# Unread identity products behind the work that precedes TensorE's pauses, in a two-block kernel on one core

## Chip, core and metric

The kernel runs on one core of one Trainium2 chip. The metric is the device time of one execution in microseconds (us). TensorE (PE) multiplies, VectorE (DVE) and ScalarE (ACT) do elementwise work and empty the product banks, GpSimd (POOL) takes powers, and SyncE (SP) issues the transfers from memory.

## What is computed

The input is 256 positions of width 1024, in float32. A first block mixes (RWKV recurrence, gated linear recurrence), attends to a memory of 256 rows and ends in a convolutional feed-forward layer. A second block does this twice: feed-forward, three-branch token mixing, cross attention, feed-forward. Each step starts from a normalised input:

```python
x = x + merged @ w_mix_out[l]
x = x + cross_attention(rms_norm(x, norm_x_g[l]), rms_norm(mem, norm_mem_g[l]), w_cq[l], w_ckv[l], w_co[l])
x = x + conv_ffn(rms_norm(x, norm_ffn_g[l]), ...)
...
for l in range(DEPTH_2):
    x = x + 0.5 * rms_norm_2(swiglu(h, ffn1_w13[l], ffn1_w2[l]), ffn1_norms[l, 1])
    x = x + rms_norm_2(y, mix_norms[l, 1])                               # y: token mixing
    x = x + rms_norm_2(cross_attention_2(h, m, cross_wq[l], cross_wkv[l], cross_wo[l]), cross_norms[l, 1])
    x = x + 0.5 * rms_norm_2(swiglu(h, ffn2_w13[l], ffn2_w2[l]), ffn2_norms[l, 1])
```

## The kernel before

All weights stream once from memory. `weights` (L213) loads one 512 KB tile `raw`; ACT casts it to a rounded half `wh` (L209) and DVE subtracts to get the rest `wl` (L210). Activations are kept as such pairs too (`xth`, `xtl`). `mm3` (L240) then makes each product from three: high by high, high by low, low by high (L242 to L244). Tiles `raw`, `wh` and `wl` come from rings of buffers, of three each in most steps.

Product banks are of 128 by 512 numbers. `bank` (L132) gives them out from two rings of two: tag `p` for projections (`bp` in the profile), tag `c` for transposes and attention (`bc`). A ring is handed out in the order in which the program is written: the third request waits until the first bank's last user is through. The four accumulators of a down projection (`acc`) are separate.

`norm_T` (L355) opens each step. It normalises the two tiles of 128 positions, `xn` on DVE (L351), and transposes them (L368) with the constant identity `ident` on TensorE, eight transposes to a tile, four to a `bc` bank; ACT and DVE empty each bank into `xth` and `xtl`. Only then can the step's projections run.

What TensorE does meanwhile is set by the scheduler: it simulates the program and queues, engine by engine, what it finds ready, so work that stands later in the code can go ahead of work that waits. In `cross` (L492) this is the projection of the memory (keys and values, `w_ckv` or `cross_wkv`, written after `norm_T`): chunks that were not made in an earlier step, 48 products each with 512 columns. There are two such chunks in the first block and one in each of the two layers of the second. Feed-forward steps are given projections of the memory as `fill`, except the very last one, which has none.

`rwkv` (L643) does the recurrence for two halves of the heads. At the end of each half it transposes the result `yc` (L868); ACT and DVE then scale it, add to it, and split it into `zh` and `zl`, which the branch projection reads.

Of the kernel before, what the change touches and what calls it, by code (L numbers as in the profile page):

```python
# [8 lines left out]
F32 = mybir.dt.float32  # L9
# [7 lines left out]
D = 1024  # L17
# [93 lines left out]
class Core:  # L111
# [87 lines left out]
    def setup(self):  # L199
        nc = self.nc  # L200
        self.x0 = self.load_x(self.a["x"][0], lambda: setattr(self, "g0", self.gvec(self.a["norm_mix_g"][0])))
        self.load_const(["ident"])
        self.ident = self.cst["ident"]
        self.mhalf = self.const.tile([128, 8], F32, name="mhalf")
        nc.vector.memset(self.mhalf, -0.5)


    def split(self, src, h, l):
# [31 lines left out]
    def mm3(self, out, a, b, start, stop):  # L240
        mm = self.nc.tensor.matmul
        mm(out, a.h, b.h, start=start, stop=False, skip_group_check=True)  # L242
        mm(out, a.h, b.l, start=False, stop=False, skip_group_check=True)  # L243
        mm(out, a.l, b.h, start=False, stop=stop, skip_group_check=True)  # L244

    def mm(self, out, a, b, start=True, stop=True):
        self.nc.tensor.matmul(out, a, b, start=start, stop=stop, skip_group_check=True)  # L247

    def fm_pair(self, b, name, bufs):

# [25 lines left out]
    def down(self, acc, t, hid, w, first, last):  # L276
        for half in range(2):
            s = slice(half * 512, (half + 1) * 512)
            self.mm3(acc[t][:, s], hid[:, t * 128:(t + 1) * 128], w[:, s], first, last)

    def down_steps(self, src, nk, pool, ntail):

# [69 lines left out]
                                                op0=ALU.mult, op1=ALU.mult)  # L352
        return xn

    def norm_T(self, xs, gsrc, dst=None, g=None):  # L355

        nc = self.nc
        g = g or self.gvec(gsrc)
        xns = [self.normed(xs[t], g) for t in range(2)]
        xt = dst  # L360
        for t, xn in enumerate(xns):
            if xt is None:
                xt = [Pair(self.s4([128, 4, T], F32R, "xth"), self.s4([128, 4, T], F32R, "xtl")) for _ in range(2)]
            for half in range(2):
                b = self.bank("c")
                for j in range(4):
                    k = half * 4 + j
                    nc.tensor.transpose(b[:, j * 128:(j + 1) * 128], xn[:, k * 128:(k + 1) * 128], self.ident)  # L368
                d = xt[half][:, :, t * 128:(t + 1) * 128]
                self.last_copy = self.split(b.rearrange("p (k c) -> p k c", k=4), d.h, d.l)  # L370
        return [xt[k // 4][:, k % 4, :] for k in range(KD)]
# [31 lines left out]


    def ffn(self, xs, gsrc, w_in, w_out, hidden, fill=None):
        xt = self.norm_T(xs, gsrc)
        if fill:
            self.parts = PK
            fill()
        self.parts = PF  # L410
        pend = []
        with self.pool("ff", 3) as pool, self.pool("tail", FTAIL) as tail, self.pool("raws", 7) as raws:
            self.phase(pool)
            acc, step = self.down_steps(w_out, 2 * NJ, tail, FTAIL)
            for j in range(NJ + 1):
                self.raws = raws if j else self.wp
                if j < NJ:
                    bg = self.proj_fm(self.wcols(w_in, j * 256, 256), xt)
                    bu = self.proj_fm(self.wcols(w_in, FF + j * 256, 256), xt)
                    hd = hidden(j, bg, bu)  # L420
                    if j == 0:
                        self.R("gap0", [128, 48], bufs=1)
                    p = Pair(self.R("hh", [128, 2, T], F32R), self.R("hl", [128, 2, T], F32R))
                    if j == 0:
                        self.R("gap1", [128, 16], bufs=1)
                    self.split(hd, p.h, p.l)
                    pend.append(p)
                if j:
                    for i in range(2):
                        step(2 * (j - 1) + i, pend[j - 1][:, i, :])  # L430
        self.raws = self.wp
        return acc
# [59 lines left out]
    def cross(self, xs, gx, w_q, w_o, mt, w_kv, raw, mid=None, ntail=TAIL):  # L492

        nc = self.nc
        self.parts = PC
        R = self.R
        xt = self.norm_T(xs, gx)
        after = self.last_copy
        kv = {}

        def get(i):

            got = []
            if i in raw:
                for r in raw[i]:
                    p = Pair(R("kvh", [128, 2, T], F32R, 8), R("kvl", [128, 2, T], F32R, 8))
                    with self.tc.issue_after(after):
                        self.split(r, p.h, p.l)
                    got.append([p[:, 0, :], p[:, 1, :]])
            else:  # L510
                got = [self.fm_pair(b, "kv", 8) for b in self.kv_chunk(mt, w_kv, i)]
            if i < 4:
                kv[i] = got[0]
            else:
                for j in range(2):
                    kv[2 * i - 4 + j] = [got[0][j], got[1][j]]

        outs = {}
        sc, pt = {}, {}

        def scores(h):
            if h == 0:
                R("gap0", [128, 16], bufs=1)
            q = self.fm_pair(self.proj_fm(self.wcols(w_q, h * 256, 256), xt), "cq", 2)
            b = self.bank("c")
            v = b.rearrange("p (a c) -> p a c", a=2)
            for t in range(2):
                for i in range(2):
                    self.mm3(v[:, t, :], q[i][:, t * 128:(t + 1) * 128], kv[h][i], t == 0 and i == 0, t == 1 and i == 1)
            p, rc = self.softmax_bank(v, 2, 256 ** -0.5, R("p", [128, 2, T], bufs=4))  # L530
            for t in range(2):
                nc.vector.tensor_scalar(out=p[:, t, :], in0=p[:, t, :], scalar1=rc[:, t:t + 1], scalar2=None,
                                        op0=ALU.mult)
            sc[h] = p

        def values(h):
            p = sc[h]
            b = self.bank("c")
            for kt in range(2):
                for t in range(2):  # L540
                    o = kt * T + t * 128
                    nc.tensor.transpose(b[:, o:o + 128], p[:, t, kt * 128:(kt + 1) * 128], self.ident)
            if h == 0:
                R("gap1", [128, 96], bufs=1)
            pt = self.fm_pair(b, "pt", 2)
            if h == 0:
                R("gap2", [128, 16], bufs=1)
            b = self.bank("c")
            for i in range(2):
                for kt in range(2):  # L550
                    self.mm3(b[:, i * T:(i + 1) * T], kv[4 + h][kt][:, i * 128:(i + 1) * 128], pt[kt],
                             i == 0 and kt == 0, i == 1 and kt == 1)
            outs[h] = self.fm_pair(b, "kv", 8)

        for i in range(6):
            if i not in raw:
                get(i)
        for h in range(4 + LAG):
            if h < 4:
                for i in (h, 4 + h // 2):  # L560
                    if i in raw and (i < 4 or h % 2 == 0):
                        get(i)
                scores(h)
            if h >= LAG:
                values(h - LAG)
        if mid:
            mid()
        return self.down_all([outs[h][i] for h in range(4) for i in range(2)], w_o, ntail)
# [74 lines left out]
    def rwkv(self, lup, krv, hf, zp):  # L643


        nc, cst, vec, mm = self.nc, self.cst, self.vec, self.mm
# [13 lines left out]
        uc = lambda u: slice(u * 128, (u + 1) * 128)  # L660
# [9 lines left out]
        t, m, y, cl = t01[:, 0], t01[:, 1], t2c[:, 0], t2c[:, 1]  # L670
# [194 lines left out]
        V.tensor_tensor(out=yc, in0=yc, in1=rs.unsqueeze(2).to_broadcast([128, 8, 64]), op=ALU.mult)  # L865
        b = W()
        for q in range(4):
            nc.tensor.transpose(b[:, uc(q)], yc[:, 2 * q:2 * q + 2, :].rearrange("p h c -> p (h c)"), self.ident)  # L868
        z = self.R("i0_%d" % hf, [128, 2, T])
        for i, j in enumerate(js):  # L870
            S.activation(out=z[:, i, :].rearrange("p (a c) -> p a c", a=2),
# [99 lines left out]
    def mix1(self, gate_pool, load, early, side):  # L971

        nc, a = self.nc, self.a
        xt = self.norm_T(self.x0, None, g=self.g0)
        load(["vecs"])
        Rg = self.phase(gate_pool)
        with self.pool("m1") as pool, self.wides():
# [47 lines left out]
    def run(self, out):  # L1025
# [39 lines left out]
        with self.pool("b2") as pool:  # L1065
            self.load_const(["ret"], pool)
            for l in range(2):
# [5 lines left out]
                with self.pool("cr") as cp:  # L1073
                    self.phase(cp)
                    acc = self.cross(xs, n2[l, 0], a["cross_wq_2"][l], a["cross_wo_2"][l], mem["mt"],
                                     a["cross_wkv_2"][l], mem["raw"], mid=(lambda: prepare(1)) if l == 0 else side.close, ntail=TAILS[l])
                xs = self.residual(xs, acc, n2[l, 1])
                acc = self.ffn(xs, a["ffn2_norms_2"][l, 0], a["ffn2_w13_2"][l], a["ffn2_w2_2"][l], self.swiglu_hidden,
                               (lambda: fill(2)) if l == 0 else None)
# [382 lines left out]
```

## Time and profile before

| | before |
|---|---|
| median of 3 runs | 2061.27 us |
| lowest and highest | 2055.84 and 2065.23 us |
| profiled execution, its own time | 2056.62 us |
| its span from first to last instruction | 2054.8 us |
| TensorE busy | 1994.9 us (97% of the span), 14508 products |
| DVE, ACT busy | 1320.3 us (64%), 1093.4 us (53%) |
| mean granted TensorE clock | 0.993 |
| share of TensorE in the chain that ended last | 86% |

A row of the time line gives start, duration, engine, line, operation, output and inputs, and how many were merged (x); in brackets stands the idle time before it and what ended it. Durations of products overlap, so what a product costs in a stream is the distance from start to start. The granted clock is 1.00 at 2.4 GHz and 0.50 at 1.2 GHz.

### The profile page before, as it was taken

How to read it: one execution, taken by the hardware profiler on the slowest of the kernel's cores; microseconds unless marked ns; L12 is line 12 of the kernel's file. 1: busy time of each engine (PE TensorE's matmuls, PEld its weight loads, DVE VectorE, ACT ScalarE, POOL GpSimd, SP SyncE). 2: the span in 40 equal slices, each digit the busy share in tenths (PEclk: the TensorE clock that was granted, in tenths of full speed). 3: DMA queues.
4: the chain of work that ended last, by engine and by line, in shares of the span. 5: the costliest groups of instructions: out<-in, count | busy, mean ns of one | idle time of the engine just before them, and what ended most of it. 6: DMA issues, size and time to landing. Idle time of an engine off the chain costs nothing.

```text
span 2054.8 us, 36137 instructions
## 1 busy us (share of the span) xinstructions
PE 1994.9 (97%) x14508; PEld 1831.4 (89%) x14508; DVE 1320.3 (64%) x2183; ACT 1093.4 (53%) x2014; POOL 45.4 (2%) x65
## 2 busy tenths in 40 slices
PE   7999999999999999999999999999999999998998
PEld 6989978899999998789988999999987899888997
DVE  6896566766675566666677655655576656765555
ACT  5763345655564456654456544544466544554444
POOL 0000000000000001000000000000000000000000
PEclk9999999999999999999999999999999999999999
DMA  6432255666666654436665666656635456645663
GB/s 200 145 120 85 90 188 181 224 189 187 186 217 190 193 174 144 138 113 175 200 203 182 218 194 196 204 184 190 196 117 154 122 159 187 204 154 174 194 193 106
DMA packets 259033, 352.92 MB, mean 172 GB/s; under 512 B 12336, under 2 KB 214448, under 8 KB 258864
## 3 DMA queue, kind: packets, MB, share of 16 engines
q1 hardware_dynamic: 258864, 350.60, 55.3%
q8 instruction: 114, 1.87, 0.4%
q14 instruction: 55, 0.45, 0.1%
HBM read 349.50 MB, written 1.05 MB: 171 GB/s over the span
## 4 chain that ended last, share of the span: by engine, by line
PE 86%; DVE 6%; ACT 3%; DMA 3%; issue 1%; POOL 0%; SPq 0%; DVEq 0%; POOLq 0%; ACTq 0%
PE bp L242 20%; PE bp L243 20%; PE bp L244 19%; PE acc L242 6%; PE acc L243 6%; PE acc L244 6%; PE a L247 3%; DVE wl L210 2%; ACT wh L209 1%; PE bc L247 1%; DMA raw<-in_w_in_dram 1%; PE bc L368 1%; DMA raw<-in_cross_wkv_dram 1%; PE bc L1137 1%; DMA raw<-in_cross_wo_dram 1%
## 5 line engine op out<-in xcount | busy, mean ns | idle before, releaser
L210 DVE TENSOR_TENSOR wl<-raw,wh 128x512 fp32r<-128x512 f32 (+2 forms) x1082 | 797.0, 774 | 523.0 <-ACT wh L209 512.4
L209 ACT CAST wh<-raw 128x512 fp32r<-128x512 f32 (+2 forms) x1082 | 699.7, 688 | 701.4 <-PE bp L243 486.6
L242 PE MATMUL bp<-xth,wh 128*128 128x256 f32 x2704 | 759.7, 281 | 8.1 <-ACT xth L209 4.8
L244 PE MATMUL bp<-xth,wl 128*128 128x256 f32 x2704 | 756.5, 280 | 5.5 <-DVE wl L210 5.4
L243 PE MATMUL bp<-xtl,wh 128*128 128x256 f32 x2704 | 756.8, 280 | 2.7 <-DVE xtl L210 2.7
L242 PEld LDWEIGHTS bp<-xth,wh 128*128 128x128 f32 x2704 | 512.4, 190 | 19.6 <-ACT xth L209 6.4
L244 PEld LDWEIGHTS bp<-xth,wl 128*128 128x128 f32 x2704 | 511.7, 189 | 11.3 <-DVE wl L210 6.9
L243 PEld LDWEIGHTS bp<-xtl,wh 128*128 128x128 f32 x2704 | 511.2, 189 | 6.8 <-DVE xtl L210 4.0
L243 PE MATMUL acc<-wl,hh 128*128 128x512 f32 x440 | 172.9, 393 | 0.0
L244 PE MATMUL acc<-wh,hl 128*128 128x512 f32 x440 | 170.9, 391 | 0.0
L242 PE MATMUL acc<-wh,hh 128*128 128x512 f32 x440 | 142.7, 393 | 0.0
L242 PE MATMUL bp<-wh,xth 128*128 128x512 f32 (+1 forms) x256 | 98.7, 400 | 2.3 <-DVE tmd L1132 1.4
L243 PE MATMUL bp<-wl,xth 128*128 128x512 f32 (+1 forms) x256 | 100.5, 396 | 0.0
L244 PE MATMUL bp<-wh,xtl 128*128 128x512 f32 (+1 forms) x256 | 99.2, 393 | 0.0
L244 PEld LDWEIGHTS acc<-wh,hl 128*128 128x128 f32 x440 | 82.7, 188 | 15.0
L243 PEld LDWEIGHTS acc<-wl,hh 128*128 128x128 f32 x440 | 82.8, 188 | 14.3
L242 PEld LDWEIGHTS acc<-wh,hh 128*128 128x128 f32 x440 | 79.2, 188 | 14.1
L343 POOL TENSOR_TENSOR rr<-rv,mhalf 128x1 f32<-128x1 f32 x46 | 30.1, 656 | 1644.8 <-DVE rv L341 1644.3
L242 PEld LDWEIGHTS bp<-wh,xth 128*128 128x128 f32 x256 | 47.3, 188 | 13.3 <-ACT tmd L1282 2.2
L243 PEld LDWEIGHTS bp<-wl,xth 128*128 128x128 f32 x256 | 48.2, 188 | 9.2 <-DVE wl L210 0.8
L244 PEld LDWEIGHTS bp<-wh,xtl 128*128 128x128 f32 x256 | 48.2, 188 | 8.4
L244 PE MATMUL bp<-bh,wl 128*128 128x256 f32 x192 | 54.0, 281 | 0.0
(377 smaller groups left out, 2578.7 us busy)
## 6 DMA issues: line engine op xcount, KB each, us to landing
raw<-in_ffn_w_dram SPq DMA_DIRECT2D x264, 512.0 KB, 4.4
raw<-in_w_in_dram SPq DMA_DIRECT2D x134, 512.0 KB, 3.7
raw<-in_w_ffn_in_dram SPq DMA_DIRECT2D x44, 512.0 KB, 4.6
raw<-in_cross_wkv_dram SPq DMA_DIRECT2D x32, 512.0 KB, 4.4
raw<-in_w_branch_dram SPq DMA_DIRECT2D x24, 512.0 KB, 3.8
raw<-in_w_ffn_out_dram SPq DMA_DIRECT2D x22, 512.0 KB, 4.2
raw<-in_w_ckv_dram SPq DMA_DIRECT2D x16, 512.0 KB, 4.7
raw<-in_w_out_dram SPq DMA_DIRECT2D x16, 512.0 KB, 4.2
```

The costliest lines, as they stand in the source:

```text
L209: first = self.nc.scalar.copy(out=h, in_=src)
L210: self.nc.vector.tensor_tensor(out=l, in0=src, in1=h.bitcast(F32), op=ALU.subtract)
L242: mm(out, a.h, b.h, start=start, stop=False, skip_group_check=True)
L243: mm(out, a.h, b.l, start=False, stop=False, skip_group_check=True)
L244: mm(out, a.l, b.h, start=False, stop=stop, skip_group_check=True)
L247: self.nc.tensor.matmul(out, a, b, start=start, stop=stop, skip_group_check=True)
L343: nc.gpsimd.tensor_tensor(out=r, in0=v, in1=self.mhalf[:, :1], op=ALU.pow)
L368: nc.tensor.transpose(b[:, j * 128:(j + 1) * 128], xn[:, k * 128:(k + 1) * 128], self.ident)
L1137: self.nc.tensor.transpose(b[0:s.shape[1], i * 128:(i + 1) * 128], s, self.ident)
```

## The change

A new helper `busy` writes products of 128 by 128 into a bank that nobody reads, `ident` by `ident` or ones by ones, by the plain `mm`. It is put at these places:

- in `setup`, 24 products of ones, before anything else;
- in `norm_T`, where asked, after the eighth transpose of each tile: 6 and 2 in the first mixing step and in the feed-forward step without fill (the last one), 4 and 1 in the three cross attentions;
- in `rwkv`, 14 after the last half's transposes;
- in `run`, 22 after the down projection of the last cross attention.

The banks are of ring `p`, except in `setup` and `rwkv`, where they are of ring `c`.

```diff
+        ones = self.s4([128, D], F32, "ones")[:, 0:128]
+        nc.vector.memset(ones, 1.0)
+        self.busy(24, "c", ones)
...
+    def busy(self, n, tag="p", src=None, after=None):
+
+        b = self.bank(tag)
+        src = self.ident if src is None else src
+        with ExitStack() as order:
+            if after is not None:
+                order.enter_context(self.tc.issue_after(after))
+            for _ in range(n):
+                self.mm(b[:, 0:128], src, src)
...
-            self.mm3(acc[t][:, s], hid[:, t * 128:(t + 1) * 128], w[:, s], first, last)
+            self.last_down = self.mm3(acc[t][:, s], hid[:, t * 128:(t + 1) * 128], w[:, s], first, last).ins
...
-    def norm_T(self, xs, gsrc, dst=None, g=None):
+    def norm_T(self, xs, gsrc, dst=None, g=None, busy=0):
...
-                    nc.tensor.transpose(b[:, j * 128:(j + 1) * 128], xn[:, k * 128:(k + 1) * 128], self.ident)
+                    turn = nc.tensor.transpose(b[:, j * 128:(j + 1) * 128], xn[:, k * 128:(k + 1) * 128], self.ident)
+                if busy and half:
+                    self.busy(busy if t == 0 else busy // 3, after=turn.ins)
...
-        xt = self.norm_T(xs, gsrc)
+        xt = self.norm_T(xs, gsrc, busy=0 if fill else 6)
...
-        xt = self.norm_T(xs, gx)
+        xt = self.norm_T(xs, gx, busy=4)
...
+        if hf:
+            self.busy(14, "c", after=turn.ins)
...
-        xt = self.norm_T(self.x0, None, g=self.g0)
+        xt = self.norm_T(self.x0, None, g=self.g0, busy=6)
...
+                if l:
+                    self.busy(22, after=self.last_down)
```

The order in which the engines take their work moves with it. TensorE at the start of the last cross attention, before: projection of the memory (`mth`, `mtl` are its transposed halves), then transposes of the first tile. The 36 products ahead of the first transpose all read `wh`, `wl` of the memory's weights and follow directly on the accumulator products.

```order
L243 MATMUL bp_19594<-wl_19556,mth1_12123 128x512
L244 MATMUL bp_19594<-wh_19555,mtl1_12124 128x512
L368 MATMUL bc_19509<-c_ident_80,xn_19485 128x128 x4
L368 MATMUL bc_19516<-c_ident_80,xn_19485 128x128 x4
L242 MATMUL bp_19569<-wh_19563,mth1_12123 128x512
L242 MATMUL bp_19594<-wh_19563,mth1_12123 128x512
```

The same place now, from the last accumulator product on (lines are those of the changed file: L381 transposes, L250 is `mm`, L245 to L247 are `mm3`).

```order
L246 MATMUL acc11_19371<-wl_19477,mh_19354 128x512
L247 MATMUL acc11_19371<-wh_19476,ml_19355 128x512
L381 MATMUL bc_19575<-c_ident_80,xn_19551 128x128 x4
L381 MATMUL bc_19582<-c_ident_80,xn_19551 128x128 x4
L250 MATMUL bp_19587<-c_ident_80 128x128 x4
L381 MATMUL bc_19594<-c_ident_80,xn_19561 128x128 x4
L381 MATMUL bc_19601<-c_ident_80,xn_19561 128x128 x4
L250 MATMUL bp_19606<-c_ident_80 128x128
L245 MATMUL bp_19642<-wh_19612,mth0_12187 128x512
```

All transposes and the new products stand ahead of the memory's projection, of which nothing is left before them. The other two cross attentions are moved in the same way.

ACT at the program's start, before: splits of transposed tiles (`xth`) between casts of the first weights (`wh`).

```order
L209 CAST xth_110<-bc_114 128x4x128
L209 CAST wh_156<-raw_154 128x1024
L209 CAST xth_112<-bc_121 128x4x128
L209 CAST wh_162<-raw_160 128x1024
L209 CAST xth_110<-bc_128 128x4x128
L209 CAST wh_233<-raw_231 128x1024
```

ACT at the same place now.

```order
L212 CAST wh_193<-raw_191 128x1024
L212 CAST wh_199<-raw_197 128x1024
L212 CAST xth_137<-bc_141 128x4x128
L212 CAST xth_139<-bc_148 128x4x128
L212 CAST wh_270<-raw_268 128x1024
L212 CAST xth_137<-bc_162 128x4x128
```

Two casts of weights now stand ahead of the first split.

## Rows read from the trace of the kernel before

**Rows 1.** Page, busy time of engines; then TensorE's waits: total, times, longest.

```profile
PE 1994.9 (97%) x14508; PEld 1831.4 (89%) x14508; DVE 1320.3 (64%) x2183; ACT 1093.4 (53%) x2014; POOL 45.4 (2%) x65
...
PE acc L242 <- ACT kvh L209: 10.6, 9, 2.8
```

**Rows 2.** Stretches: length, busy PE, PEld, DVE, ACT, POOL (x), granted clock, DMA, GB/s.

```profile
16.64:21.30 4.66, 4.66 (x22) 4.66 (x23) 4.18 (x18) 0.44 (x1) 0.00 (x0) 1.00 0.92 265
21.30:26.00 4.70, 4.70 (x41) 4.53 (x40) 0.72 (x3) 1.33 (x2) 0.00 (x0) 1.00 0.34 115
...
268.98:273.89 4.91, 4.91 (x21) 4.68 (x22) 0.82 (x2) 0.36 (x1) 0.00 (x0) 0.50 0.00 0
1062.37:1065.78 3.41, 3.41 (x18) 3.41 (x18) 1.86 (x4) 0.02 (x1) 0.00 (x0) 0.50 1.03 403
1857.68:1867.92 10.24, 6.51 (x27) 5.69 (x28) 6.81 (x11) 3.73 (x8) 1.12 (x3) 0.50 0.67 241
```

**Rows 3.** Time line of PE at the end of `rwkv`.

```profile
265.06 0.66 PE L868 MATMUL a<-c_ident,i 128*128 128x128 f32 x4 [1.49 <-DVE i L865]
268.98 0.79 PE L242 MATMUL bp<-zh,wh 128*128 128x256 f32 x2 [3.27 <-ACT zh L209]
```

**Rows 4.** Time line of the last feed-forward step's start, DVE and PE.

```profile
1859.07 1.41 DVE L351 SCALAR_TENSOR_TENSOR xn<-x,rr,g 128x512 f32<-128x512 f32 x2
...
1859.96 1.94 PE L368 MATMUL bc<-c_ident,xn 128*128 128x128 f32 x8 [4.80 <-DVE xn L351]
1863.35 1.97 PE L368 MATMUL bc<-c_ident,xn 128*128 128x128 f32 x8 [1.45 <-DVE xtl L210]
1865.14 0.79 PE L242 MATMUL bp<-xth,wh 128*128 128x256 f32 x2
```

**Rows 5.** Last cross attention, PE: time line, then one group of 1775.85 to 1789.2.

```profile
1775.67 0.40 PE L244 MATMUL acc<-wh,ml 128*128 128x512 f32 x1
1775.91 0.40 PE L242 MATMUL bp<-wh,mth 128*128 128x512 f32 x1
...
1791.49 0.38 PE L243 MATMUL bp<-xtl,wh 128*128 128x256 f32 x1 [0.65 <-DVE xtl L210]
...
L242 PE MATMUL bp<-wh,mth 128*128 128x512 f32 x16 | 6.3, 401 | 0.0
```

**Rows 6.** Last cross attention, time line of DVE: the two normalised tiles.

```profile
1780.06 1.42 DVE L351 SCALAR_TENSOR_TENSOR xn<-x,rr,g 128x512 f32<-128x512 f32 x2 [0.43 <-DMA g<-in_cross_norms_dram]
...
1782.21 1.41 DVE L351 SCALAR_TENSOR_TENSOR xn<-x,rr,g 128x512 f32<-128x512 f32 x2 [0.66 <-POOL rr L343]
```

**Rows 7.** Cross attention of the second block's first layer, DVE and PE.

```profile
1049.86 1.41 DVE L351 SCALAR_TENSOR_TENSOR xn<-x,rr,g 128x512 f32<-128x512 f32 x2
...
1061.28 0.39 PE L243 MATMUL bp<-xtl,wh 128*128 128x256 f32 x1 [0.90 <-DVE xtl L210]
```

**Rows 8.** Cross attention of the first block, DVE and PE.

```profile
304.73 0.69 DVE L383 TENSOR_TENSOR x<-acc,x 128x512 f32<-128x512 f32 x1
305.49 1.42 DVE L351 SCALAR_TENSOR_TENSOR xn<-x,rr,g 128x512 f32<-128x512 f32 x2
...
329.52 0.39 PE L242 MATMUL bp<-xth,wh 128*128 128x256 f32 x1 [0.94 <-DVE kvl L210]
```

**Rows 9.** Plain products of 128 by 128: twelve `mm` calls of `pv_tokens` (L1145).

```profile
892.50 2.84 PE L247 MATMUL a<-vt,pt 128*128 128x128 f32 x24
```

**Rows 10.** Program's start: ACT, DVE and PE.

```profile
9.40 0.59 ACT L209 CAST xth<-bc 128x512 fp32r<-128x512 f32 x1
...
12.56 1.04 ACT L209 CAST wh<-raw 128x1024 fp32r<-128x1024 f32 x1 [0.74 <-DMA raw<-in_w_in_dram]
...
15.03 0.69 DVE L210 TENSOR_TENSOR xtl<-bc,xth 128x512 fp32r<-128x512 f32 x1
...
16.64 0.58 PE L242 MATMUL bp<-xth,wh 128*128 128x256 f32 x1 [1.07 <-ACT wh L209]
17.02 0.42 PE L243 MATMUL bp<-xtl,wh 128*128 128x256 f32 x1
```

More of the change, by code (lines that the diff above doesn't have):

```diff
@@ L243, in mm3 @@
         mm(out, a.h, b.l, start=False, stop=False, skip_group_check=True)
-        mm(out, a.l, b.h, start=False, stop=stop, skip_group_check=True)
+        return mm(out, a.l, b.h, start=False, stop=stop, skip_group_check=True)
     def mm(self, out, a, b, start=True, stop=True):
         self.nc.tensor.matmul(out, a, b, start=start, stop=stop, skip_group_check=True)
+    def busy(self, n, tag="p", src=None, after=None):
[6 more added lines that the diff above has]
+                self.mm(b[:, 0:128], src, src)
     def fm_pair(self, b, name, bufs):
@@ L867, in rwkv @@
         for q in range(4):
-            nc.tensor.transpose(b[:, uc(q)], yc[:, 2 * q:2 * q + 2, :].rearrange("p h c -> p (h c)"), self.ident)
+            turn = nc.tensor.transpose(b[:, uc(q)], yc[:, 2 * q:2 * q + 2, :].rearrange("p h c -> p (h c)"), self.ident)
+        if hf:
+            self.busy(14, "c", after=turn.ins)
         z = self.R("i0_%d" % hf, [128, 2, T])
```

## The prediction

> **What bounds the kernel now.** I read the page first: TensorE is busy for 97% of the span, 1994.9 us [rows 1]. Time can therefore come from two places only: the pauses of TensorE, and the stretches in which it works at the lower clock. I looked for the second by the stretches with their granted clock [rows 2]. At 0.50, the 1.2 GHz level, 22 products take 4.66 us at the program's start, 0.212 us each. After the rise 41 take 4.70 us, 0.115 us each. (The clock column still says 1.00 for the start; the spacing of the products shows the lower level.) So a stretch of products at the lower level costs twice its due. Three such stretches lie near edits: 268.98 to 273.89, 1062.37 to 1065.78 and the end of 1857.68 to 1867.92 [rows 2]. Ahead of the first and last lie pauses, 3.27 us [rows 3] and 4.80 us [rows 4]. Next I read the time line of the pauses, and last, against the order in which the engines take their work, who fills the time that the norms take. That reading decides: in the last cross attention TensorE goes from its last accumulator product at 1775.67 straight to the memory's projection at 1775.91 [rows 5], while DVE needs until 1780.06 to begin the first normalised tile [rows 6]. The norm's latency is hidden there, by 36 products.
>
> **The change, part by part.** I number the product of 128 by 128 first. Twelve plain products appear as 24 records with a duration of 2.84 us from first start to last end [rows 9]; less the tail of the last that is 0.22 us each at full clock, and twice that, 0.45 us, at the lower level.
>
> *End of rwkv.* The 14 products take 14 x 0.22 = 3.1 us and start when the four transposes are through, about 265.5. They end near 268.6, before `zh` allows the next real product at 268.98 [rows 3]: nothing is delayed. If the clock holds, the 4.91 us at the lower level [rows 2] become half: **-2.4 us**. Had the clock fallen before, they would take 14 x 0.45 = 6.3 us and delay by 2.9 us, which is the other end (about +0.5 net of the clock, since the run then comes out of it warm).
>
> *Last feed-forward step.* The 22 products take 4.8 us against a pause of 4.80 us [rows 4], so they neither delay nor leave a hole. The transposes after it wait for DVE's split (the 1.45 us [rows 4]), not for TensorE, so a faster clock does little for them, and 6 + 2 products fit between. What is won is the products from 1865.14 [rows 4] to the rise at 1867.92 [rows 2]: 2.78 us become 1.4: **-1.4 us**. Bounds: -2.3 (the transposes too) and +1 (products late).
>
> *Start.* The 24 products of ones start at about 1 us and end between 6.4 us (full clock) and 11.7 us (never). The first splits of `xt` cannot be hurt by that, because ACT's order now has two weight casts ahead of them, and the second of those starts at 12.56, when its transfer has landed [rows 10]. The first split stood at 9.40 [rows 10] and goes to 13.6. From there I follow the chain with DVE's durations: subtraction of both banks until 16.4, the second tile's transposes behind these, its splits on ACT after the cast that ends at 16.6, then DVE's 1.23 us weight subtraction and 0.69 us: the stream that began at 17.02 [rows 10] begins near 18.5. That is 1.5 us late; small later waits for weights give some back: **+1.0 us**, between -1.0 (the 4.66 us at the lower clock [rows 2] shortened after all) and +2.2.
>
> *The three cross attentions.* Here the change moves work. `busy` asks for a `p` bank twice inside `norm_T`, and the memory's projection, later in the code, asks for the next two. The ring has two, so these products must wait until the new ones are through, and the new ones are placed behind the transposes. The order shows it: 36 products ahead of the first transpose before, none now. They are the same products, so nothing is saved: TensorE stands while the norm runs, then makes them. The price of standing I take from the last feed-forward step, the one norm in the trace before that has no cover: from the start of `xn` at 1859.07 to the first projection at 1865.14 it takes 6.07 us, and the first transpose comes 0.89 us after `xn` [rows 4]. The second `xn` comes 2.15 us after the first in the last cross attention [rows 6] and 2.2 us in that step, so the pattern carries over.
>
> - Last cross attention: `xn` at 1780.06 [rows 6], so TensorE stands from 1775.91 to 1780.95, and the memory's 48 products (16 of each kind [rows 5]) start at 1786.1. They are 0.233 us apart (the distance of 1775.67 and 1775.91 [rows 5]), 11.2 us. The pause is as long as the one after which the clock fell [rows 4], so I charge the fall: the run at the lower level after products resume lasted 2.8 to 4.9 us [rows 2, 3, 4], of which half is lost, 1.4 to 2.4, taken 1.9. The projection of `xt` starts at 1799.2 instead of 1791.49 [rows 5]: **+7.7 us**, 5.8 if the clock holds, 8.5 with a stall for the weights behind it.
> - First layer: `xn` at 1049.86 [rows 7], products from 1055.9, 11.2 and 1.9 us, so 1069.0 against 1061.28 [rows 7], 7.7 us; the fall of the clock from 1062.37 on, which cost 3.41 / 2 [rows 2], is then not paid: **+6.0 us**, between 4 and 7.
> - First block: DVE now has the last addition, 0.6 us, ahead of `xn`, which so starts at 306.1 instead of 305.49 [rows 8]. With 6.07 us the projection starts at 312.2; with DVE's new order of the four subtractions, in which the second tile's first bank comes ahead of the first tile's second, at 313.4. Taken 312.8, then 96 products, 22.4 us, and 0.6 us for a clock that may fall: 335.8 against 329.52 [rows 8]: **+6.3 us**, between 5 and 8.5.
>
> On the clock in this last place the Trainium skill ("TensorE: Matmul & The Clock Gate", Part 4) adds a rule: transposes do not count as activity for the clock as products do. The trace agrees so far that eight transposes from 1863.35 were followed by no rise, which came 2.78 us into the products [rows 2, 4]. By the rule the first block's clock would surely fall, and its term would be 1.3 us larger; I leave it.
>
> Give-back: TensorE waits in the later parts of the cross attentions, 10.6 us over nine waits for `kvh` [rows 1]. These hang on ACT's queue, whose casts wait for buffers that TensorE's own products free, so they move along with it: taken 1, up to 4.
>
> Sum: 6.3 + 6.0 + 7.7 + 1.0 - 2.4 - 1.4 - 1 = **+16.2 us**. Against the profiled execution's own 2056.62 us that is 2072.8; that execution is 4.65 us under the median of 2061.27 and lies in the range of the three runs. The mean of all four is 2059.7, and I set the sum on that: **2076 us**.
>
> **The rivals.** *The clock and the later waits pay it back.* The standing TensorE leaves DVE, ACT and the transfers time to run ahead; the 10.6 us of waits for `kvh` [rows 1] shrink to a few, and the clock holds in all three places (-4.4). Then the sum is 16.2 - 4.4 - 5 = +7, 2067 us. For it: these waits exist; against it: the buffers that link both sides.
>
> *Ready products pass the waiting transposes.* If TensorE took the memory's products while a transpose ahead waits, nothing would be lost in the cross attentions and the gains would stand: -2.4 - 1.4 - 1.7 + 1.0 = -4.5, 2055 us; it is decided by whether the queue keeps its order at the first pause of 5 us. The trace speaks against it: the product that ran at 17.02 had its `xtl` by 15.72 and its weights before that, yet it ran behind the one that waited until 16.64 [rows 10]. The Trainium skill ("TensorE: Matmul & The Clock Gate", table at the top) has the queue as a window that pulls weight loads ahead; this case shows nothing of products doing so.
>
> *The products don't hold the clock.* Then they run at 0.45 us: 14 delay by 2.9 us, 22 by some 5 us, the gains of 3.8 go, and the first block pays the clock too: 16.2 + 2.9 + 5 + 3.8 + 1.3 = +29, 2089 us. Against it: they are plain products like those after which the clock rose.
>
> **How the numbers follow.** Forecast 0.68, pay-back 0.18, passing 0.06, no hold 0.08. A measurement of this kernel can tell 0.5%, 10.3 us, from no change: the marks are 2051 and 2071.6. The terms' low ends give 5 + 4 + 5.8 - 1 - 2.4 - 2.3 - 4 = +5, their high ends 8.5 + 7 + 8.5 + 2.2 + 0.5 + 1 = +28, not all at once. The range is 2062 to 2086: it takes in the pay-back and leaves out passing and no hold. Slower: most of the forecast (0.62) and all of no hold, with a little of pay-back, 0.72; within: the rest of forecast and pay-back and most of passing, 0.26; faster 0.02.
>
> **What would show it.** In the profile after, pauses of about 5 us (last layer), 6 us (first layer) and 3 us (first block) in front of the transposes of each cross attention, ended by `xn`; the memory's products behind the transposes in one run; the clock at 1.00 from 265 to 274 and from 1855 to 1868; the first stream of products near 18.5. Wrong would be: no such pauses (passing), or pauses but the next steps starting as early as before (pay-back), or new products 0.45 us apart in the two covered pauses.

## The result, and the profile after

The change makes the kernel slower: the median went from 2057.36 us to 2074.06 us (seven runs of each, 2055.59 to 2065.23 and 2069.59 to 2076.30), a ratio of 1.0071 with a 95% interval of 1.0057 to 1.0084. The forecast was 2076 us, and slower. The profiled execution after took 2076.30 us, with a span of 2074.5 us.

The page first, then TensorE's waits (total, times, longest), as in [rows 1].

```profile
PE 2017.4 (97%) x14690; PEld 1854.6 (89%) x14690; DVE 1321.5 (64%) x2184; ACT 1095.2 (53%) x2014; POOL 45.5 (2%) x65
...
PE bc L381 <- DVE xn L364: 13.5, 3, 5.4
PE acc L245 <- ACT kvh L212: 9.3, 9, 2.2
...
PE bp L245 <- DVE kvl L213: 3.8, 4, 0.9
```

TensorE is again 97% busy, now of a longer span: the average share says nothing. What says something is the new first line of the waits: transposes (L381) wait for `xn` three times, 13.5 us. Before, the long one of them was the 4.80 us of the last feed-forward step [rows 4]; that one is gone, and these three are the cross attentions. Their time line on TensorE, first block, first layer, last layer (last accumulator product, first transpose, first product of the memory, first product of `xt`; in the first block the memory's halves are called `xth` and `xtl` too, and its products are those with 512 columns):

```profile
300.24 0.40 PE L247 MATMUL acc<-wh,ml 128*128 128x512 f32 x1
303.56 1.32 PE L381 MATMUL bc<-c_ident,xn 128*128 128x128 f32 x8 [2.92 <-DVE xn L364]
...
310.70 0.77 PE L245 MATMUL bp<-wh,xth 128*128 128x512 f32 x1
...
325.03 0.51 PE L245 MATMUL bp<-wh,xth 128*128 128x512 f32 x1 [0.94 <-DVE kvl L213]
...
337.25 0.39 PE L245 MATMUL bp<-xth,wh 128*128 128x256 f32 x1 [0.94 <-DVE kvl L213]
...
1051.79 0.39 PE L247 MATMUL acc<-wh,ml 128*128 128x512 f32 x1
1057.31 1.97 PE L381 MATMUL bc<-c_ident,xn 128*128 128x128 f32 x8 [5.13 <-DVE xn L364]
...
1062.78 0.50 PE L245 MATMUL bp<-wh,mth 128*128 128x512 f32 x1
...
1074.99 0.38 PE L245 MATMUL bp<-xth,wh 128*128 128x256 f32 x1 [0.94 <-DVE kvl L213]
...
1788.40 0.39 PE L247 MATMUL acc<-wh,ml 128*128 128x512 f32 x1
1794.23 1.97 PE L381 MATMUL bc<-c_ident,xn 128*128 128x128 f32 x8 [5.44 <-DVE xn L364]
...
1799.69 0.67 PE L245 MATMUL bp<-wh,mth 128*128 128x512 f32 x1
...
1812.07 0.38 PE L245 MATMUL bp<-xth,wh 128*128 128x256 f32 x1 [0.94 <-DVE kvl L213]
```

In [rows 5] the accumulator product at 1775.67 was followed by the memory's product at 1775.91. Now 5.44 us of nothing stand there, and the memory's products come 5.46 us behind the first transpose. The stretches with their granted clock (columns as in [rows 2]), in the order of time: the start, the end of `rwkv`, the three cross attentions, the last feed-forward step:

```profile
1.08:8.42 7.34, 7.34 (x50) 7.34 (x51) 1.57 (x3) 2.83 (x7) 0.56 (x1) 1.00 0.88 283
...
14.94:18.36 3.42, 2.80 (x13) 2.74 (x13) 3.10 (x7) 2.22 (x3) 0.00 (x0) 0.50 1.08 355
18.36:26.00 7.64, 7.34 (x63) 7.06 (x61) 3.81 (x17) 1.66 (x2) 0.00 (x0) 1.00 0.61 148
265.00:268.30 3.30, 3.16 (x28) 2.97 (x27) 1.61 (x3) 1.50 (x3) 0.00 (x0) 1.00 0.30 119
...
305.08:315.32 10.24, 8.15 (x28) 6.49 (x27) 3.85 (x6) 1.76 (x3) 0.00 (x0) 0.50 0.03 12
...
1057.31:1062.84 5.53, 5.53 (x27) 5.49 (x27) 3.63 (x7) 1.86 (x4) 0.55 (x1) 0.50 0.70 214
...
1794.23:1800.11 5.88, 5.88 (x27) 5.85 (x28) 3.98 (x7) 2.22 (x4) 0.55 (x1) 0.50 0.12 43
1875.29:1880.36 5.07, 5.07 (x46) 5.01 (x45) 5.01 (x10) 3.50 (x12) 1.10 (x2) 1.00 0.93 305
1880.36:1888.00 7.64, 6.85 (x54) 6.02 (x54) 4.39 (x8) 2.35 (x4) 0.55 (x1) 1.00 0.56 209
```

The covers of the two old pauses, and the products behind them, are at 1.00 (2.4 GHz) now, where [rows 2] had 0.50. (The column says 1.00 for the very start as well; as in the kernel before, the spacing shows otherwise there: the products of ones are 0.43 us apart until 4.7 us, and 0.22 us after that.) The three new pauses are followed by 0.50 (1.2 GHz): the fall has moved from the places covered to the places made.

To see what each place is worth, I took every product of the old kernel in the trace, subtracted its start from the start of the same product in the other trace, and took the median of that lag in stretches between the places. What the lag grows by at a place is that place's share, in us (what a row lacks to its last column came between the places):

| execution | start | end of rwkv | first block | first layer | last layer | last feed-forward | in all |
|---|---|---|---|---|---|---|---|
| forecast | +1.0 | -2.4 | +6.3 | +6.0 | +7.7 | -1.4 | +16.2 (with -1 given back) |
| the change | -0.9 | -2.0 | +10.1 | +5.6 | +7.6 | -0.5 | +19.8 |
| e1, without the cross attentions' products | -0.3 | -2.2 | +1.5 | +0.5 | +1.0 | -0.7 | -0.4 |
| e2, these in ring `c` | -0.8 | -1.3 | -0.5 | -0.2 | -0.3 | -1.3 | -4.5 |
| e3, two banks of `p` alone | -1.1 | -0.1 | +9.0 | +6.6 | +6.3 | -0.3 | +20.3 |
| e4, new pauses filled too | -1.2 | -1.4 | +7.3 | +7.3 | +5.8 | -0.7 | +17.0 |
| e5, e2 with the later waits filled | +1.6 | -1.3 | +1.5 | -1.1 | +1.1 | -0.7 | +1.0 |
| e6, ring `c` products alone | -0.7 | +0.1 | +1.3 | -1.7 | +0.4 | +0.1 | -0.5 |
| e7, rwkv and last feed-forward alone | +2.0 | -1.3 | -0.9 | -0.5 | -0.4 | -0.7 | -1.0 |
| e8, start alone | -1.6 | -0.7 | -0.5 | -0.1 | +0.4 | +0.6 | -2.0 |
| e9, e7 with e6 | +2.8 | -1.3 | -1.0 | -2.1 | +0.1 | -0.8 | -2.3 |
| e10, e7 once more | +0.2 | -2.2 | -1.3 | +0.4 | +0.3 | -0.7 | -3.3 |

Each row is one execution. Its columns can be off by 1 to 2 us, at the start by up to 3 us, even where nothing was edited (e7 and e10 are one kernel, without the start's products: +2.0 and +0.2 at the start). Terms of that size are read from several rows, and the verdict on a kernel from its ratio.

### The profile page after: what moved, and what is told of

It is laid out like the page before. It is cut to its first block, busy times and chain, and to the rows that moved or that the text cites. A ratio compares the mean times of both kernels' runs of the same rounds, so it can differ in the third digit from the quotient of the medians.

```text
span 2074.5 us, 36505 instructions
## 1 busy us (share of the span) xinstructions
PE 2017.4 (97%) x14690; PEld 1854.6 (89%) x14690; DVE 1321.5 (64%) x2184; ACT 1095.2 (53%) x2014; POOL 45.5 (2%) x65
## 4 chain that ended last, share of the span: by engine, by line
PE 87%; DVE 5%; ACT 3%; DMA 3%; issue 1%; POOL 0%; SPq 0%; DVEq 0%; POOLq 0%; ACTq 0%
PE bp L245 20%; PE bp L246 20%; PE bp L247 20%; PE acc L245 6%; PE acc L246 6%; PE acc L247 6%; PE a L250 4%; DVE wl L213 2%; ACT wh L212 2%; PE bc L250 1%; PE bc L381 1%; DMA raw<-in_cross_wkv_dram 1%; PE bc L1156 1%; DMA raw<-in_w_in_dram 1%; DMA g<-in_cross_norms_dram 1%
## 5 line engine op out<-in xcount | busy, mean ns | idle before, releaser
L245 PE MATMUL bp<-xth,wh 128*128 128x256 f32 x2704 | 757.9, 281 | 5.4 <-DVE kvl L213 2.8
L247 PE MATMUL bp<-xth,wl 128*128 128x256 f32 x2704 | 754.7, 280 | 4.8 <-DVE wl L213 4.8
L245 PEld LDWEIGHTS bp<-xth,wh 128*128 128x128 f32 x2704 | 510.2, 189 | 16.5 <-DVE kvl L213 4.1
L247 PEld LDWEIGHTS bp<-xth,wl 128*128 128x128 f32 x2704 | 508.9, 188 | 10.4 <-DVE wl L213 6.0
L247 PE MATMUL acc<-wh,hl 128*128 128x512 f32 x440 | 170.9, 391 | 0.0
L245 PE MATMUL acc<-wh,hh 128*128 128x512 f32 x440 | 142.8, 393 | 0.0
L245 PE MATMUL bp<-wh,xth 128*128 128x512 f32 (+1 forms) x256 | 99.7, 404 | 2.7 <-DVE tmd L1151 1.4
L247 PE MATMUL bp<-wh,xtl 128*128 128x512 f32 (+1 forms) x256 | 99.5, 395 | 0.0
L247 PEld LDWEIGHTS acc<-wh,hl 128*128 128x128 f32 x440 | 82.7, 188 | 15.1
L245 PEld LDWEIGHTS acc<-wh,hh 128*128 128x128 f32 x440 | 79.2, 188 | 14.1
L245 PEld LDWEIGHTS bp<-wh,xth 128*128 128x128 f32 x256 | 47.9, 190 | 14.2 <-ACT tmd L1301 2.2
L381 PE MATMUL bc<-c_ident,xn 128*128 128x128 f32 x224 | 37.4, 307 | 21.4 <-DVE xn L364 13.5
L247 PEld LDWEIGHTS bp<-wh,xtl 128*128 128x128 f32 x256 | 48.7, 190 | 8.6
```

The lines of the kernel that those rows point to most:

```text
L247: return mm(out, a.l, b.h, start=False, stop=stop, skip_group_check=True)
L381: turn = nc.tensor.transpose(b[:, j * 128:(j + 1) * 128], xn[:, k * 128:(k + 1) * 128], self.ident)
```

## The experiments

**Is it the cross attentions, and there the ring?** Four kernels were run beside the kernel before. The first drops the products there:

```diff
-        xt = self.norm_T(xs, gx, busy=4)
+        xt = self.norm_T(xs, gx)
```

> The changed kernel without the unread products in the three cross attentions; all its other places stay (start, end of rwkv, last feed-forward step). Theory (the two banks taken from ring p move the memory's projection behind the norm): TensorE again makes 36 of the memory's products ahead of the first transpose of the second block's cross attentions, the pauses of 2.9 to 5.4 us there are gone, and what is left are the other terms as the changed kernel's trace shows them, about -2.1 at the end of rwkv, -1.1 at the last feed-forward step and -1 to 0 at the start: 2052 to 2055 us where before is 2057, ratio 0.998 (0.996 to 0.9995). Rival 1 (the loss in the cross attentions has another cause, for instance their transfers or the later waits): 2068 us or more. Rival 2 (the other places cost too): over 2060 us.

Measured: 2056.19 us, ratio 0.9988 (0.9977 to 0.9999). The waits for `xn` are gone from the list, and the rest is a small gain; theory met, both rivals out.

The second keeps the five products of each place, but takes their banks from the other ring:

```diff
+                    self.busy(busy if t == 0 else busy // 3, tag, after=turn.ins)
...
+        xt = self.norm_T(xs, gx, busy=4, tag="c")
```

> The changed kernel with the same unread products in the cross attentions (4 and 1), but their bank taken from ring c instead of ring p; nothing left out. Theory (it is the ring, not the products): the memory's products stand ahead of the transposes again; the five products per step, 1.1 us of TensorE at most in each of three places, and a later transfer of a c bank cost 1 to 4 us together: 2053 to 2058 us, ratio 0.998 to 1.001. Rival (the products or their place behind the transposes cost the time): as slow as the changed kernel, 2070 to 2076 us.

Measured: 2053.19 us, ratio 0.9974 (0.9962 to 0.9985). The same products, placed behind the same transposes, and by the ratios (1.0071 and 0.9974) some 20 us less than the change. Its time line on TensorE in the last cross attention shows why: the memory's products run right up to the transposes, which wait for nothing; the unread products come later, behind the rest of the memory's.

```profile
1780.92 0.40 PE L246 MATMUL bp<-wl,mth 128*128 128x512 f32 x1
1781.15 0.40 PE L247 MATMUL bp<-wh,mtl 128*128 128x512 f32 x1
1781.39 1.03 PE L381 MATMUL bc<-c_ident,xn 128*128 128x128 f32 x8
...
1785.13 1.16 PE L250 MATMUL bc<-c_ident 128*128 128x128 f32 x8
```

The third is the reverse: the kernel before with two banks of ring `p` taken in each cross attention, one product in each, and nothing else of the change.

```diff
-                    self.busy(busy if t == 0 else busy // 3, after=turn.ins)
+                    self.busy(1, after=turn.ins)
```

> The kernel before, with one unread product in each of two p banks in every cross attention, and nothing else of the change. Theory: the two banks alone carry the whole loss of the cross attentions, read as +10.4, +4.9 and +8.5 us by place, with up to 1 us of it given back: less 3 x 3 x 0.22 = 2 us for the products that are fewer, +20 us, 2077 us, ratio 1.0095 (1.008 to 1.0115). Rival (the unread products carry it): four of five are gone, so under +6 us, 2063 us.

Measured: 2080.22 us, ratio 1.0105 (1.0084 to 1.0125). Two products of 0.22 us per place bring the whole loss (four runs, all of them slower than the slowest of the kernel before). On TensorE in the first layer:

```profile
1059.05 1.97 PE L378 MATMUL bc<-c_ident,xn 128*128 128x128 f32 x8 [6.17 <-DVE xn L361]
1060.81 0.63 PE L247 MATMUL bp<-c_ident 128*128 128x128 f32 x2
1062.46 1.97 PE L378 MATMUL bc<-c_ident,xn 128*128 128x128 f32 x8 [1.02 <-DVE xtl L210]
...
1064.51 0.77 PE L242 MATMUL bp<-wh,mth 128*128 128x512 f32 x1
```

With e1 to e3 this is settled: the two banks are the cause, and neither the products in them nor their place. A bank asked for in `norm_T` stands ahead of the memory's in the ring, its user waits for the transposes, and so the memory's products wait for the norm.

**How much of the loss is the clock?** The fourth fills the new pauses as well:

```diff
+        self.busy(24, after=self.last_down)
         xt = self.norm_T(xs, gx, busy=4)
```

> The changed kernel with 24 more unread products in front of each cross attention's norm, behind the last product of the down projection ahead of it, so that TensorE is busy in the new pause. Theory (of the loss, the fall of the clock is a part, the missing cover by the memory's products the rest): the clock stays at 1.00 through 300 to 316, 1051 to 1063 and 1788 to 1800; each place wins half of what runs at 0.50 there, 2.3 us in the first block, 2 to 2.8 in the others: 2067 us (2065 to 2070), ratio 1.005. Rival 1 (the clock is the whole loss): back to 2055 us. Rival 2 (the products don't hold the clock, or are late): 2074 us or more.

Measured: 2070.24 us, ratio 1.0056 (1.0039 to 1.0074). The three places (columns as above) are at full clock:

```profile
298.00:315.00 17.00, 15.45 (x105) 13.82 (x104) 11.26 (x20) 7.32 (x16) 1.12 (x2) 1.00 0.31 97
1049.00:1064.00 15.00, 12.70 (x91) 11.22 (x91) 9.78 (x18) 6.33 (x16) 2.38 (x4) 1.00 0.56 180
1787.00:1801.00 14.00, 12.29 (x90) 10.89 (x89) 11.11 (x21) 6.86 (x19) 2.75 (x4) 1.00 0.34 122
```

But the ratio moves by 1.0071 - 1.0056 = 0.0015, 3 us, not the 7 us that I expected, and the intervals overlap. So the traces speak for the clock as the small part of the loss and the norm without cover as the large one; four runs of e4 do not measure the small part by time. In the first block 2.8 us came back, in the last layer 1.8; in the first layer nothing did, since there the norm itself came later: `xn` waited for the vector `g`, in the change 0.40 us, in e4 1.64 us (DVE, change first, then e4).

```profile
1056.51 1.41 DVE L364 SCALAR_TENSOR_TENSOR xn<-x,rr,g 128x512 f32<-128x512 f32 x2 [0.40 <-DMA g<-in_cross_norms_dram]
```

```profile
1055.34 1.41 DVE L364 SCALAR_TENSOR_TENSOR xn<-x,rr,g 128x512 f32<-128x512 f32 x2 [1.64 <-DMA g<-in_cross_norms_dram]
```

**Is a pause that no work can fill worth covering?** In the cross attentions' later part TensorE waits for `kvh`, and the clock falls. To e2 I added ten products there, in the second block:

```diff
+                    turn = self.mm3(b[:, i * T:(i + 1) * T], kv[4 + h][kt][:, i * 128:(i + 1) * 128], pt[kt],
...
+            if h == 1 and mid:
+                self.busy(10, "c", after=turn.ins)
```

> The kernel of the run with the cross attentions' unread products in ring c, and 10 more unread products (ring c) behind the second head's last values product in the cross attentions of the second block, where TensorE waits for the cast of kvh (2.59 us and 2.34 us in that run) and the clock falls each time. Theory (a pause that nothing useful can fill is worth covering): the products, 10 x 0.22 = 2.2 us, lie in the waits, the clock stays at 1.00 around 1097 to 1101 and 1828 to 1831, each place wins half of 3.41 us: 3.4 us less than 2053.2, about 2050 us, ratio 0.9957 (0.9945 to 0.9972). Rival 1 (the products push back the transposes of p and with them ACT's casts, the wait grows): 2053 us or more, ratio 0.9975 or more. Rival 2 (what follows waits for weights, the faster products wait later): as before, 2053 us.

Measured: 2056.15 us, ratio 0.9995 (0.9985 to 1.0005): no gain over e2, rather a loss. The theory fell. TensorE in the first layer, then in the last, there with ACT's cast that the pause was a wait for:

```profile
1098.05 2.50 PE L250 MATMUL bc<-c_ident 128*128 128x128 f32 x20
1100.60 0.50 PE L245 MATMUL acc<-wh,kvh 128*128 128x512 f32 x1
...
1829.74 0.58 ACT L212 CAST kvh<-bc 128x512 fp32r<-128x512 f32 x1
1829.89 4.13 PE L250 MATMUL bc<-c_ident 128*128 128x128 f32 x20 [1.95 <-ACT p L501]
1833.78 0.48 PE L245 MATMUL acc<-wh,kvh 128*128 128x512 f32 x1
```

In the first layer they lie in the wait, as meant. In the last they wait 1.95 us for ACT's `p` to release their own bank of ring `c`. ACT goes straight from there to the awaited cast of `kvh`, which ends at 1830.32, 0.43 us after the cover's first product. The cover then runs for 4.13 us, most of it at the lower clock (0.50 from 1830.28 to 1833.69), and pushes the awaited product back to 1833.78. So the cover waited for the same stretch of ACT's queue as the product that it was to cover for. What makes e5 slower than e2 beyond that one place was not separated.

**The small parts.** The five products in ring `c` alone:

```diff
+        xt = self.norm_T(xs, gx, busy=4, tag="c")
```

> The kernel before with the five unread products of each cross attention in ring c and nothing else of the change. Theory A (they do nothing; the 2.9 us between the run without them and the run with them in ring c is chance): 2057 to 2061 us, ratio 0.9993 to 1.0008. Theory B (they hold the clock behind the transposes): no stretch at 0.50 near 1062 and 1792, 1.7 us won at the first of these, ratio 0.9980 to 0.9992. Theory C (they cost their own time, 3 x 1.1 us): ratio 1.0015.

Measured: 2056.35 us, ratio 0.9994 (0.9985 to 1.0002): worth nothing that can be told. Theory C is out; A and B are not told apart, since most executions without these products have no fall of the clock near 1062 either.

The products at the end of `rwkv` and in the last feed-forward step alone, run twice:

```diff
+        xt = self.norm_T(xs, gsrc, busy=0 if fill else 6)
...
+        if hf:
+            self.busy(14, "c", after=turn.ins)
...
+                if l:
+                    self.busy(22, after=self.last_down)
```

> The kernel before with the 14 products at the end of rwkv and the 22, 6 and 2 of the last feed-forward step; nothing at the start, nothing in the cross attentions. Theory (the start's products are worth nothing, because a transfer of weights sets the time at 110 us anyway): -2.0 at the end of rwkv and -0.5 to -1.3 at the last step, ratio 0.9983 to 0.9993, as the run with the start's products too. Rival (the start's edit costs its 1 us): ratio 0.9980 or less, and the first 100 us of the trace earlier than there by 1 us.

> The products at the end of rwkv and in the last feed-forward step alone, once more, beside the two other kernels: 0.9976 (0.9967 to 0.9985) if the first value holds; 0.9985 or more if it was a lucky draw and these two places bring only the -2.0 and -0.5 us that the traces show.

Measured: 2053.18 us, 0.9976 (0.9967 to 0.9985), then 2054.08 us, 0.9989 (0.9980 to 0.9998). Both are gains. The first lies below the theory's range, where the rival (the start costs 1 us) had put it; the second lies on the side of the lucky draw, and the run of the start alone (below) does not bear out the rival. The mean, 0.9982, is 3.6 us, a little over the 2 to 3 us that the places show.

The start alone:

```diff
+        ones = self.s4([128, D], F32, "ones")[:, 0:128]
+        nc.vector.memset(ones, 1.0)
+        self.busy(24, "c", ones)
...
+        xt = self.norm_T(self.x0, None, g=self.g0, busy=6)
```

> The kernel before with the start's edits alone: 24 products of ones at the very start, 6 and 2 behind the first step's transposes. Theory (the first 110 us end at a wait for weights, so a lower or a higher clock and a later first split there change nothing): ratio 0.9996 to 1.0004. Rival (the start costs 1 to 2.5 us, as the run with all three other edits against the run without the start's suggests, 0.9988 against 0.9976): ratio 1.0005 to 1.0015.

Measured: 2056.89 us, ratio 1.0003 (0.9995 to 1.0011). The start is worth nothing that can be told, though the interval does not exclude the lower half of the rival's range. The reason that the theory gave is not what the traces show. TensorE does wait 3.52 us near 110 us, in the change as in the kernel before, but 1.17 us earlier there: the wait moves along with what stands ahead of it and makes up nothing. The change, then the kernel before:

```profile
109.48 0.39 PE L247 MATMUL bp<-xth,wl 128*128 128x256 f32 x1 [3.52 <-DVE wl L213]
```

```profile
110.65 0.58 PE L244 MATMUL bp<-xth,wl 128*128 128x256 f32 x1 [3.52 <-DVE wl L210]
```

By the lags, the first products do come late, by 1.3 to 1.8 us at 17 to 18 us in all six executions with the start's products, and what becomes of that is settled by 24 us. Where the granted clock is back at 1.00 by 18.3 to 18.9 us (the change, e2, e4, e8; in the kernel before the spacing falls at 21.30 [rows 2]), nothing of it is left: the products are 0.0 to 0.5 us early. In e1 and e5, where it stays at 0.50 until 21.03 and 21.21, they are 0.7 and 1.0 us late. The executions without the start's products lie between -0.5 and +0.4 us there.

Last, e7's edits with the products in ring `c`:

```diff
+        xt = self.norm_T(xs, gx, busy=4, tag="c")
...
+            self.busy(14, "c", after=turn.ins)
...
+                    self.busy(22, after=self.last_down)
```

> The kernel before with the products at the end of rwkv and in the last feed-forward step, and those of the cross attentions in ring c; nothing at the start. If the parts add up (0.9976 for the first two, 0.9994 for the third): 0.9970 (0.9960 to 0.9980), about 2052 us. Rival (the third part is worth nothing): 0.9976 as without it.

Measured: 2052.80 us, ratio 0.9977 (0.9967 to 0.9987). It is faster than the kernel before and than the change, and not to be told from e2 (0.9974) or e7, so it does not show that the parts add up; the simplest that wins is e7, without any product in the cross attentions or at the start.

## Why the prediction was right

**The sum.** +16.2 us forecast; the medians differ by 16.7 us, the ratio gives 14.6 us (11.7 to 17.3), and the two profiled executions, of which the later was the longest of its seven, differ by 19.8 us. That the sum comes so close is luck in part: by place the first block is 3.8 us above its term and the start 1.9 us below, and every column carries the scatter of its one execution.

**What bounds the kernel, and the moved work.** Right, and decisive: the order of the queues told of three new pauses, and [rows 5, 6] told what had filled them. Pauses of 5, 6 and 3 us were forecast; 5.44, 5.13 and 2.92 us came.

**Last and first layer.** +7.7 forecast, +7.6 read; +6.0 forecast, +5.6 read. The step from [rows 4], 6.07 us from `xn` to the first projection in a norm without cover, carried over: 1062.78 - 1056.51 = 6.27 us in the first layer, and 1799.69 - 1793.42 = 6.27 us in the last, where `xn` stands at:

```profile
1793.42 1.42 DVE L364 SCALAR_TENSOR_TENSOR xn<-x,rr,g 128x512 f32<-128x512 f32 x2 [1.07 <-DMA g<-in_cross_norms_dram]
```

Errors cancel in the two terms. I let the lower clock hit the memory's products (1.9 us); in truth it was spent almost wholly on transposes and unread products, and rose 0.06 and 0.42 us into the memory's. Against that I left out a wait of 0.94 us for `kvl` behind them, and in the last layer `xn` waits 1.07 us for `g` instead of 0.43 [rows 6]. The 1.7 us that I took as saved in the first layer were no property of the kernel (last section).

**First block.** +6.3 forecast, +10.1 read: the one term outside its bounds (5 to 8.5). I gave the 96 products 22.4 us, from start to start in a stream. They took 337.25 - 310.70 = 26.55 us: 22.4, two waits of 0.94 us for `kvl` (in the time line above; one of them was in [rows 8] already), and 2.3 us for 4.6 us at 0.50, where I had put 0.6. The start, at 310.70, is with the 2.9 us by which everything was ahead there 0.8 us later than the 312.8 that I worked out. The clock fell here, 0.50 from 305.08 to 315.32, so the 1.3 us that I left out belonged in the term. The rule of the Trainium skill ("TensorE: Matmul & The Clock Gate", Part 4), that transposes do not count as activity for the clock as products do, had pointed to this fall. No run here shows that the transposes are its reason: in e4 the same transposes stand behind a pause filled with products, and the stretch is at 1.00.

**The gains.** End of `rwkv`: -2.4 forecast; read -2.0 in the change, and over the eight executions with the cover -2.0 to -2.2 in three and -1.3 or -1.4 in five, against -0.7 to +0.1 without. The two values are two clocks: in the five the granted clock is 0.50 for 3.4 us, from at most 0.5 us before the cover's first product on; in the three it stays at 1.00. TensorE in the change and in e7:

```profile
264.66 3.29 PE L250 MATMUL bc<-c_ident 128*128 128x128 f32 x28
268.09 0.50 PE L245 MATMUL bp<-zh,wh 128*128 128x256 f32 x2
```

```profile
267.57 4.92 PE L247 MATMUL bc<-c_ident 128*128 128x128 f32 x28
272.25 0.48 PE L242 MATMUL bp<-zh,wh 128*128 128x256 f32 x2
```

In e7 the clock had fallen as the cover began (0.64 on average over its 4.68 us), the products took 4.92 us instead of 3.29 and delayed the real one by 1.25 us: the other end that the prediction named (2.9 us), less than half as large. Last feed-forward step: -1.4 forecast, -0.5 to -1.3 read. The mechanism held (22 products in 5.07 us, no hole, clock 1.00), and so did the size at the place itself: by some 5 us after the first projection the lag has moved by -1.3 to -1.5 us in all eight executions with the cover. What I had not reckoned with comes behind it. In seven of the eight, 0.6 to 0.8 us are lost again within 30 us, in products that stand 0.118 us apart instead of 0.113 at the same granted clock, without a wait. The same 20 us of products, in the kernel before and in the change (columns as in [rows 2]):

```profile
1868.00:1888.00 20.00, 20.00 (x176) 19.91 (x176) 8.87 (x14) 10.08 (x17) 0.00 (x0) 1.00 0.39 120
```

```profile
1887.00:1907.00 20.00, 20.00 (x170) 19.91 (x169) 8.87 (x14) 9.74 (x16) 0.00 (x0) 1.00 0.39 114
```

In e2 the spacing stays at 0.113, and there the -1.3 us are kept. The cover alone is not the reason, since e8, which has none here, loses 0.6 us in the same way; what sets the spacing stays open.

**Start.** +1.0 forecast, nothing that can be told measured (e8), -0.9 read in the change. The delay of the first stream did come (the product at 17.02 [rows 10] stands at 18.66, forecast 18.5). The step that failed is to let most of it last: the clock was back at 1.00 from 18.36 on, and by 22 us the products were 0.2 us early. That is the lower bound that the prediction names, the 4.66 us at the lower level shortened after all; it should have been the term.

**The rivals.** Pay-back did not come: the waits for `kvh` went from 10.6 [rows 1] to 9.3 us, 1.3 us where I had taken 1; without the new pauses they are 10.3 us in e2 and 11.6 in e1, so even this is within the scatter. That products don't hold the clock is out by the stretches above, though at the end of `rwkv` the clock fell as the cover began in five of eight executions. Passing is out as a forecast, since TensorE stood; whether ready products could pass a waiting transpose was not tried by itself, since here the banks barred them too.

## What to carry to other kernels

A buffer taken from a ring is a place in a queue: ask who asks for the next ones, and what that work was hiding, before adding even a product that nobody reads. A pause that real work fills is not a pause; cover only those that the trace shows as empty, with a buffer that is free when the pause begins. Two such covers won 3.6 us of 2057 here. And sum a stream with the waits that stand between its parts, not by its spacing alone.

## What was not expected

- The cover itself can run at the lower clock: in five of eight executions with the 14 products the clock fell as they began, behind a wait of 1.5 us, and two fifths of the gain went (-1.3 instead of -2.1 us).
- Whether the clock falls behind a short pause differed from execution to execution. The fall at 1062 in [rows 2] is in no other execution here that has the memory's products in front: in these it came near 1097 to 1100, or not at all. The 1.7 us that the forecast took as saved in the first layer are such a draw.
- In the first layer the vector `g`, copied to all 128 partitions (512 KB by the profile's account), takes 4.4 us from issue to landing in the kernel before, 5.7 in the change and 6.9 in e4, each time issued right behind two tiles of weights on the same queue. Why it differs was not tried. Behind the memory's products nobody sees that; without them it added up to 1.64 us to the pause.
